# Loads of x alternating between two DMA rings in a rotary-embedding kernel

## The chip, the cores and the metric

One core of one Trainium2 chip. Times are device microseconds of whole executions; the profile's span is some 1.8 us shorter. The kernels of one round run on the same chip as the kernel before; the rounds used several chips, so compare ratios rather than medians.

In the profiles VectorE is DVE, ScalarE is ACT, GpSimd is POOL, TensorE is PE and SyncE is SP. A ring is the queue of transfers that one engine has issued, q1 for SyncE and q10 for ScalarE; the core's 16 DMA engines work on both. The granted clock is the share of its full clock at which TensorE was let run.

## The reference

```python
half = x.shape[-1] // 2                     # x: (8, 8, 1024, 64) float32
x_first, x_second = x[..., :half], x[..., half:]
out_first  = x_first * cos_cached - x_second * sin_cached   # tables: (1024, 32)
out_second = x_first * sin_cached + x_second * cos_cached
return concatenate([out_first, out_second], axis=-1)
```

16.8 MB come in, 16.8 MB go out; the tables are 128 KB each.

## The kernel before

x is cut into 16 chunks of 1 MiB, c0 to c15, each 128 partitions by 2048 values. All of x fits in SBUF, so every load has its own tile and none waits for a buffer. They are issued at the start, all on SyncE's ring, behind the sine table:

```python
nc.sync.dma_start(out=sn[0:Q], in_=sin_cached...)
nc.scalar.dma_start(out=cs[0:Q], in_=cos_cached...)
xt = []
for first, n in [(0, 1), (1, 1)] + [(c, 2) for c in range(2, n_ch, 2)]:
    t = xp.tile([P, n, F], fp32, name=f"x{first}")
    nc.sync.dma_start(out=t, in_=xf[first:first + n].rearrange("c p m -> p c m"))
    xt += [t[:, i] for i in range(n)]
```

So c0 and c1 are loads of one chunk, then come seven pairs. The tables are copied to all partitions (VectorE makes `snp`, ScalarE `csp`, GpSimd its own `sn` and `cs`). Then the chunks are dealt out (cuts marked by ...):

```python
vector_tensor(0); on_pool(1); vector_pool(2); vector_pool(3); vector_tensor(4)
on_pool(6); vector_pool(5); vector_tensor(7); vector_pool(8); ...
vector_tensor(11); vector_pool(12); vector_pool(13); vector_pool(14, ...); vector_alone(15)
```

VectorE makes two products for every chunk but c1 and c6, which GpSimd does alone. One product goes to a buffer `vs` (six of them), the other overwrites x. The sums are made by GpSimd (`vector_pool`, stored through SyncE), by TensorE with ScalarE copying them out of the PSUM tile `acc` (`vector_tensor`, stored through ScalarE), or by VectorE (`vector_alone`, only c15, whose product goes to `acc`).

## Time and profile before

| | before |
|---|---|
| median of 6 runs | 86.13 us (85.78 to 86.45) |
| profiled span | 84.2 us |
| VectorE, GpSimd busy | 84%, 85% |
| HBM traffic | 33.82 MB, mean 402 GB/s |
| first VectorE product, last VectorE instruction ends | 8.87, 77.19 us |
| last store lands | 83.1 us |

Read it from both ends. In the middle both the DMA engines and VectorE are full, so it isn't plain which of them sets the time. At the end VectorE is done six us before the last store has landed.

### The profile page before, as it was taken

How to read it: one execution, taken by the hardware profiler on the slowest of the kernel's cores; microseconds unless marked ns; L12 is line 12 of the kernel's file. 1: busy time of each engine (PE TensorE's matmuls, PEld its weight loads, DVE VectorE, ACT ScalarE, POOL GpSimd, SP SyncE). 2: the span in 40 equal slices, each digit the busy share in tenths (PEclk: the TensorE clock that was granted, in tenths of full speed). 3: DMA queues.
4: the chain of work that ended last, by engine and by line, in shares of the span. 5: the costliest groups of instructions: out<-in, count | busy, mean ns of one | idle time of the engine just before them, and what ended most of it. 6: DMA issues, size and time to landing. Idle time of an engine off the chain costs nothing.

```text
span 84.2 us, 363 instructions
## 1 busy us (share of the span) xinstructions
PE 40.1 (48%) x80; PEld 15.7 (19%) x80; DVE 70.4 (84%) x34; ACT 15.7 (19%) x16; POOL 71.4 (85%) x38
## 2 busy tenths in 40 slices
PE   0000005994930896895949497794949600000000
PEld 0000002422400341423314051332414100000000
DVE  0199997999999999999999982999999999996000
ACT  4399000004040003104040402204040310000000
POOL 3199999999999999999999999999999999970000
PEclk9999999999999569999999999999999999555555
DMA  3899999999999999999999999999999999999991
GB/s 29 282 432 409 420 420 436 417 409 420 436 428 409 417 428 432 432 424 409 421 436 436 432 421 417 424 424 436 432 432 432 413 421 428 428 436 407 432 419 55
DMA packets 4736, 33.82 MB, mean 402 GB/s; under 512 B 448, under 2 KB 448, under 8 KB 768
## 3 DMA queue, kind: packets, MB, share of 16 engines
q1 hardware_dynamic: 3824, 27.40, 78.7%
q10 hardware_dynamic: 912, 6.42, 18.1%
HBM read 17.04 MB, written 16.78 MB: 402 GB/s over the span
## 4 chain that ended last, share of the span: by engine, by line
POOL 53%; DVE 23%; issue 9%; DMA 4%; DVEq 1%; POOLq 0%
POOL x L94 13%; POOL x L93 11%; DVE vs L88 11%; POOL x L89 11%; POOL gs L88 11%; DVE x L89 8%; POOL sn L77 4%; DMA sn<-in_sin_cached_dram 4%; POOL cs L77 3%; DVE acc L88 3%; DVE x L93 1%; DVEq L170 1%; POOLq L93 0%; POOLq L77 0%
## 5 line engine op out<-in xcount | busy, mean ns | idle before, releaser
L119 PE MATMUL acc<-x,plus 128*128 128x512 f32 x40 | 23.3, 666 | 26.4 <-DVE x L89 13.6
L89 DVE TENSOR_TENSOR x<-x,csp 128x2048 f32<-128x2048 f32 x14 | 32.0, 2287 | 0.6
L88 DVE TENSOR_TENSOR vs<-x,snp 128x2048 f32<-128x2048 f32 x13 | 29.7, 2282 | 2.2 <-POOL x L94 1.7
L122 ACT COPY x<-acc 128x1024 f32<-128x1024 f32 x10 | 10.1, 1012 | 49.2 <-PE acc L120 49.2
L94 POOL TENSOR_TENSOR x<-x,vs 128x1024 f32<-128x1024 f32 (+1 forms) x9 | 19.0, 2108 | 0.0
L93 POOL TENSOR_TENSOR x<-x,vs 128x1024 f32<-128x1024 f32 (+1 forms) x9 | 18.9, 2105 | 0.0
L119 PEld LDWEIGHTS acc<-x,plus 128*128 128x128 f32 x40 | 7.5, 208 | 39.4 <-issue 23.9
L120 PE MATMUL acc<-vs,minus 128*128 128x512 f32 x20 | 11.6, 666 | 0.0
L120 PE MATMUL acc<-vs,plus 128*128 128x512 f32 x20 | 10.2, 592 | 0.0
L89 POOL TENSOR_TENSOR x<-x,cs 128x2048 f32<-128x2048 f32 x2 | 9.1, 4546 | 0.2
L88 POOL TENSOR_TENSOR gs<-x,sn 128x2048 f32<-128x2048 f32 x2 | 9.1, 4542 | 0.1
L73 DVE COPY snp<-sn 32x1024 f32<-32x1024 f32 x4 | 4.9, 1223 | 3.9 <-DMA sn<-in_sin_cached_dram 3.8
L120 PEld LDWEIGHTS acc<-vs,minus 128*128 128x128 f32 x20 | 4.4, 219 | 5.9 <-issue 5.9
L77 POOL COPY sn<-sn 32x1024 f32<-32x1024 f32 x3 | 3.1, 1032 | 2.7 <-DMA sn<-in_sin_cached_dram 2.6
L93 POOL TENSOR_TENSOR x<-x,gs 128x1024 f32<-128x1024 f32 x2 | 4.7, 2362 | 0.2
L94 POOL TENSOR_TENSOR x<-x,gs 128x1024 f32<-128x1024 f32 x2 | 4.7, 2357 | 0.0
L120 PEld LDWEIGHTS acc<-vs,plus 128*128 128x128 f32 x20 | 3.8, 190 | 4.8 <-issue 4.8
L74 ACT COPY csp<-cs 32x1024 f32<-32x1024 f32 x4 | 4.0, 1008 | 1.5 <-DMA cs<-in_cos_cached_dram 1.4
L77 POOL COPY cs<-cs 32x1024 f32<-32x1024 f32 x3 | 3.1, 1033 | 0.1
L88 DVE TENSOR_TENSOR acc<-x,snp 128x2048 f32<-128x2048 f32 x1 | 2.3, 2297 | 0.0
L71 ACT ACT_TABLE_LOAD x1 | 1.3, 1283 | 1.2 <-PEq L159 1.2
L93 DVE TENSOR_TENSOR x<-x,acc 128x1024 f32<-128x1024 f32 x1 | 1.2, 1223 | 0.0
(8 smaller groups left out, 2.4 us busy)
## 6 DMA issues: line engine op xcount, KB each, us to landing
x<-in_x_dram SPq DMA_DIRECT2D x7, 2048.0 KB, 25.0
out_dram<-x SPq DMA_DIRECT2D x9, 1024.0 KB, 13.0
out_dram<-x ACTq DMA_DIRECT2D x6, 1024.0 KB, 9.0
x<-in_x_dram SPq DMA_DIRECT2D x2, 1024.0 KB, 6.3
out_dram<-x SPq DMA_DIRECT2D x2, 512.0 KB, 6.0
cs<-in_cos_cached_dram ACTq DMA_DIRECT2D x1, 128.0 KB, 3.4
sn<-in_sin_cached_dram SPq DMA_DIRECT2D x1, 128.0 KB, 3.1
```

The costliest lines, as they stand in the source:

```text
L71: nc.scalar.mul(minus, plus, -1.0)
L73: nc.vector.tensor_copy(out=snp[r * Q:(r + 1) * Q], in_=sn[0:Q])
L74: nc.scalar.copy(out=csp[r * Q:(r + 1) * Q], in_=cs[0:Q])
L77: nc.gpsimd.tensor_copy(out=t[r * Q:(r + 1) * Q], in_=t[0:Q])
L88: eng.tensor_tensor(out=rows(s), in0=xr, in1=tab(stab), op=TT.mult)
L89: eng.tensor_tensor(out=xr, in0=xr, in1=tab(ctab), op=TT.mult)
L93: eng.tensor_tensor(out=xr[:, :, 0], in0=xr[:, :, 0], in1=sr[:, :, 1], op=TT.subtract)
L94: eng.tensor_tensor(out=xr[:, :, 1], in0=xr[:, :, 1], in1=sr[:, :, 0], op=TT.add)
L119: nc.tensor.matmul(a[:, k], plus, xr[:, :, k], start=True, stop=False)
L120: nc.tensor.matmul(a[:, k], plus if k else minus, sr[:, :, 1 - k], start=False, stop=True)
L122: nc.scalar.copy(out=xr, in_=a.rearrange("p k n j -> p n k j"))
L170: with _tile.TileContext(nc) as tc:
```

## The change

Its intent: two rings instead of one for the loads, so that the issues are spread over two engines and ACT's ring, nearly idle at first, carries half. The tables stay first on their rings.

```diff
     xt = []
-    for first, n in [(0, 1), (1, 1)] + [(c, 2) for c in range(2, n_ch, 2)]:
+    loads = [(0, 1), (1, 1)] + [(c, 2) for c in range(2, n_ch, 2)]
+    for i, (first, n) in enumerate(loads):
         t = xp.tile([P, n, F], fp32, name=f"x{first}")
-        nc.sync.dma_start(out=t, in_=xf[first:first + n].rearrange("c p m -> p c m"))
+        (nc.scalar if i % 2 else nc.sync).dma_start(
+            out=t, in_=xf[first:first + n].rearrange("c p m -> p c m"))
         xt += [t[:, i] for i in range(n)]
```

## The prediction

> **What bounds the kernel now.** I read the page's slices first, then the DMA issues, then VectorE in order of time, then the end. The work is 16 chunks of x of 1 MiB each (call them c0 to c15), in nine loads: c0, c1, then pairs (c2+c3, c4+c5, ... c14+c15). From part 2 of the page:
>
> ```profile
> DVE  0199997999999999999999982999999999996000
> POOL 3199999999999999999999999999999999970000
> DMA  3899999999999999999999999999999999999991
> GB/s 29 282 432 409 420 420 436 417 409 420 436 428 409 417 428 432 432 424 409 421 436 436 432 421 417 424 424 436 432 432 432 413 421 428 428 436 407 432 419 55
> ```
>
> The DMA engines are full from the second slice to the last but one, at 410 to 436 GB/s, so no other ring can move bytes faster: 33.82 MB at some 425 GB/s are 79.6 of the 84.2 us. But VectorE (DVE) is also full from the sixth slice to the 37th, apart from one hole, and GpSimd (POOL) beside it. Two bounds lie a few us apart, and what matters is when the first chunks arrive, because every us that VectorE loses early has to be found again.
>
> The issue of the second and third pair's loads, from the timeline of SyncE (start, duration), and their landings from the DMA view of the same moments (last number: us from issue to landing):
>
> ```profile
> 2.11 0.43 SPq L65 DMA_DIRECT2D x<-in_x_dram  x1
> 2.58 0.67 SPq L65 DMA_DIRECT2D x<-in_x_dram  x1
> ```
> ```profile
> x<-in_x_dram SPq DMA_DIRECT2D x1, 2048.0 KB, 11.9
> x<-in_x_dram SPq DMA_DIRECT2D x1, 2048.0 KB, 16.3
> ```
>
> So c2+c3 land at 2.11 + 11.9 = 14.0 and c4+c5 at 2.58 + 16.3 = 18.9. The same view gives c0 at 1.18 + 5.3 = 6.5, c1 at 1.64 + 7.4 = 9.0, c6+c7 at 23.9, c8+c9 at 28.8. One ring delivers in the order of issue, a pair every 4.9 us. VectorE's timeline shows how close that runs to need:
>
> ```profile
> 8.87 2.29 DVE L88 TENSOR_TENSOR vs<-x,snp 128x2048 f32<-128x2048 f32 x1
> 11.26 2.29 DVE L89 TENSOR_TENSOR x<-x,csp 128x2048 f32<-128x2048 f32 x1
> 13.99 2.29 DVE L88 TENSOR_TENSOR vs<-x,snp 128x2048 f32<-128x2048 f32 x1 [0.44 <-DMA x<-in_x_dram]
> ...
> 51.98 2.29 DVE L88 TENSOR_TENSOR vs<-x,snp 128x2048 f32<-128x2048 f32 x1 [1.74 <-POOL x L94]
> ```
>
> VectorE multiplies c0 from 8.87, is done at 13.55 and takes c2 as it lands (0.44 us late). From there it works without a hole, two products of 2.29 us a chunk, but for 1.74 us before 51.98: there it reuses a buffer of `vs` that GpSimd frees at 51.95 (c5's sums). The last thing in the program is c15's store, from ScalarE's timeline and the DMA view:
>
> ```profile
> 77.22 0.34 ACTq L97 DMA_DIRECT2D out_dram<-x  x1
> ```
> ```profile
> out_dram<-x ACTq DMA_DIRECT2D x1, 1024.0 KB, 5.9
> ```
>
> It lands at 83.1, and the program ends 1.0 us later. In the last four us the DMA engines clear what was left of the other stores, then c15.
>
> **What the Trainium skill says.** "DMA: Bandwidth & Descriptors", section "Rules for kernel authors", says of spreading DMAs over the issuing engines for bandwidth that it "Doesn't help", it only saves issue time. The trace agrees as far as it goes: one ring alone holds 420 to 436 GB/s, and SyncE's issues cost 0.4 to 0.7 us each while the transfers take 4.9. The same page, section "Queues, rings and completion order", says that each DMA engine goes round its rows packet by packet. So two rings with work should get half each. Here is the stretch from 28.6 to 33.0 us, loads on SP's ring (q1) and c0's store on ACT's (q10), DMA view (packets, MB, share):
>
> ```profile
> q10 hardware_dynamic: 119, 0.97, 52.2%
> q1 hardware_dynamic: 112, 0.92, 49.2%
> ```
>
> Half and half: it agrees, and this is the fact on which the prediction rests. The same page, "Anatomy of one DMA", puts a fixed cost of some 2 us beside the bytes; the trace's own number is below.
>
> **The change, step by step.** It removes and adds no transfer. c0, c2+c3, c6+c7, c10+c11, c14+c15 stay on SP; c1, c4+c5, c8+c9, c12+c13 go to ACT.
>
> 1. *Arrivals.* The first loads now run side by side in twos. c0 and c1, 2 MiB together, are done when the second was before: both at about 9.0 instead of 6.5 and 9.0. VectorE wants c0 at 8.87, so it loses 0.1 us. Then c2+c3 share with c4+c5: both land when the later one did, 18.7 to 18.9. c2 thus comes 4.8 us later. c6+c7 and c8+c9 come at 28.8, c10 to c13 at about 39: all before anyone wants them (GpSimd takes c6 at 33.4; VectorE would reach c8 at 41.5 and c10 at 50.5).
>
> 2. *VectorE's new hole.* Free at 13.6, it gets c2 at 18.8: a wait of 5.2 us where there were 0.44, a shift of 4.8.
>
> 3. *What is taken back.* GpSimd's own order hardly notices: it takes c1 from 10.44 (landed 9.0, and sn and cs are copied until 10.36), c2's sums at 24.26 (products then done at 18.8 + 4.6 = 23.4), c3's at 28.8 (28.0), c6 at 33.4, c5 at 47.3. So c5's sums still end at 51.95, and VectorE, which would come to that buffer at 50.24 + 4.8 = 55.0, no longer waits there. 1.74 us are absorbed: the shift of c11 to c15 is 3.1. GpSimd's c12, c13, c14 follow VectorE closely (c12's products end at 61.11, its sums start at 61.19) and move by 3.0 too.
>
> 4. *TensorE and ScalarE.* Their chunks c4, c7, c9, c11 run back to back, two copies of 1.01 us and two gaps of 3.79 each, 9.6 us a chunk, from c4's products on. They shift by 4.8: the last copy ends at 67.57 + 4.8 = 72.4. VectorE's c15 needs that PSUM tile at 70.18 + 3.1 = 73.3. It holds by 0.9.
>
> 5. *Issues on ScalarE.* Four issues of some 0.45 us now precede its table load (1.28) and copies of cs (4.13 in all). The fourth may have to wait for a semaphore in use: before, the seventh load's issue took until 6.5 and the eighth's until 11.2. If it waits for the tables (4.1), the csp copies end at 10.3, before VectorE's second product at 11.26: nothing. If it waits for c0 (9.0), they end at about 15, the second product at about 17.3: inside the hole of step 2, still nothing.
>
> 6. *The end.* VectorE ends at 77.19 + 3.1 = 80.3, and c15's store goes out at 80.35. Before, this store queued behind others. Now the queue is nearly dry: at 425 GB/s a chunk takes 2.47 us, and by 68.9, when c12's store goes out, the engines have done some (68.9 - 3.1) / 2.47 = 26.7 of the 32.25 chunks of traffic, with 27.25 on offer (16 loads, 0.25 of tables, 11 stores). From there they wait for work. For a lone 1 MiB I take c0's load: 5.3 us from issue, less 0.6 for the 256 KB of tables ahead of it, 4.7. So c15 lands between 84.4 (bytes start 1.0 after issue, 0.5 after the last one) and 80.35 + 4.7 = 85.1, against 83.1: plus 1.3 to 1.9.
>
> Sum: 4.8 lost, 1.7 taken back at the buffer, about 1.5 taken back from the store queue at the end; plus 1.6. 86.06 + 1.6 = 87.6 us, 1.8% more.
>
> **The rivals.** *Nothing moves (86.1).* "DMA bound, same bytes": for it, the DMA row of nines. Against it, c2's wait is visible already and VectorE has only 1.74 us of idle time from there on. It would come true if loads went to one ring first, c2 landing near 14. *The change pays (84 to 85).* It would have to come from SyncE's issues, which block until 11 and 15 us; but the ring is full then and the bytes flow at 425. c1 earlier would help GpSimd, but it starts on its table copies' end. I give this almost nothing. *A heavier loss (89 to 95).* If ScalarE's queue is held by a load's issue until c2 lands, csp is done only near 25, and VectorE shifts another 8. Or ACT's stores, now behind ACT's loads, hold back a semaphore or an issue that the PE chain needs; step 4 has 0.9 to spare. Possible, not likely.
>
> **Range and chances.** Step 2 is worth 4 to 5, depending on how evenly the rings share; step 6 takes back 1 to 2. That makes +0.7 to +2.4, and I widen the upper side for step 5: 86.7 to 88.9. The limit of 2% is 87.78, just above my middle: 0.42 slower, 0.56 within, 0.02 faster.
>
> **What would show it.** In the profile after: VectorE's wait for x before c2 about 5 us, starting 13.6; loads of the first two pairs landing within 0.3 us of each other near 18.8; no wait for GpSimd near 52; c15's store issued at 80.3; DMA under 9 tenths in slices near 73 and 80 us. The prediction fails if c2 lands near 14 (rings not shared), if ScalarE's csp copies come after 15, or if the last store lands later than 4.8 us after its issue.

## More of the kernel before

The chain that ended last, by engine, is from the page:

```profile
POOL 53%; DVE 23%; issue 9%; DMA 4%; DVEq 1%; POOLq 0%
```

It runs through GpSimd's work until 52 us and then through VectorE's. It stops at the last instruction and says nothing of the DMA queue behind the stores; for that one needs the row of DMA slices.

## The result, and the profile after

87.26 us (median of 6, 86.89 to 87.34) against 86.13 of the same rounds. The ratio is 1.0121 (95% interval 1.0089 to 1.0154). The change is slower, clear of the noise but by less than 2%, and inside the predicted range (86.7 to 88.9).

The page's slices after, the same rows as in the prediction:

```profile
DVE  0299993019999999999999999999999999999600
POOL 3199899999999999999999999999708999997000
DMA  2999999999999999999999999999999998699992
GB/s 56 310 424 431 416 412 427 427 420 431 427 408 420 424 420 427 431 424 404 424 431 431 427 424 427 431 424 431 431 431 431 431 427 377 289 393 422 379 408 85
```

VectorE has a hole in slices 7 to 9 (12.8 to 19.2 us) that wasn't there, and none any more in the middle. (GpSimd's new one, 2.9 us before 64.1, is its wait for c12's products, which VectorE now makes later.) The DMA engines are as full as before from the third slice on, at 404 to 431 GB/s (before 407 to 436), until the slices from 70 to 75 us, where they run short (289 GB/s at the worst). No bandwidth was won at the start; some was lost at the end.

The second and third pair's loads are now issued at the same moment, from SyncE's and ScalarE's timeline, and these are their landings in the DMA view:

```profile
1.65 0.43 SPq L66 DMA_DIRECT2D x<-in_x_dram  x1
```
```profile
1.66 0.46 ACTq L66 DMA_DIRECT2D x<-in_x_dram  x1
```
```profile
x<-in_x_dram SPq DMA_DIRECT2D x1, 2048.0 KB, 17.1
x<-in_x_dram ACTq DMA_DIRECT2D x1, 2048.0 KB, 18.7
```

c2+c3 land at 1.65 + 17.1 = 18.7 instead of 14.0. c4+c5 land at 20.4 instead of 18.9. Neither pair came sooner. (Only c12+c13, 40.3 instead of 41.1, and c14+c15, 46.0 instead of 48.8, did, long before they were wanted.) What the two rings moved from 5 to 18.7 us, in the DMA view (packets, MB, share):

```profile
q10 hardware_dynamic: 385, 2.91, 50.8%
q1 hardware_dynamic: 386, 2.90, 50.6%
```

It is half each. In the kernel before, q1 alone moved 5.78 MB in the same stretch. VectorE's timeline (start, duration, in brackets the idle time before and what ended it):

```profile
8.88 2.29 DVE L90 TENSOR_TENSOR vs<-x,snp 128x2048 f32<-128x2048 f32 x1
11.28 2.29 DVE L91 TENSOR_TENSOR x<-x,csp 128x2048 f32<-128x2048 f32 x1
18.75 2.29 DVE L90 TENSOR_TENSOR vs<-x,snp 128x2048 f32<-128x2048 f32 x1 [5.18 <-DMA x<-in_x_dram]
...
54.92 2.28 DVE L90 TENSOR_TENSOR vs<-x,snp 128x2048 f32<-128x2048 f32 x1
```

c0 is worked on at the same time as before. c2 starts at 18.75 instead of 13.99, 4.76 later. c11 starts at 54.92 instead of 51.98 and has no wait before it: 1.8 of the 4.76 has been absorbed. VectorE's last instruction ends at 80.12, 2.93 later than before. The last store, from ScalarE's timeline and the DMA view:

```profile
80.15 0.34 ACTq L99 DMA_DIRECT2D out_dram<-x  x1
```
```profile
out_dram<-x ACTq DMA_DIRECT2D x1, 1024.0 KB, 3.9
```

It lands at 84.0, 3.9 us after its issue where it took 5.9, because less is queued ahead of it: beside c15's own 1.05 MB SyncE's ring moved 0.20 MB from 80.2 us to the end, where before it moved 1.00 MB from 77.5 us on. That gives back another 2.0, and 0.9 of the 4.76 is left in the profile. The chain that ended last names the culprit now, in its summary by engine:

```profile
DVE 60%; DMA 20%; issue 11%; DVEq 1%; SPq 1%
```

The 20% of DMA is one piece, c2+c3's load from 1.65 to 18.73; from there it is VectorE to the end. GpSimd left the chain.

### The profile page after: what moved, and what is told of

Read it like the earlier page. It is cut to its first block, busy times and chain, and to the rows that moved or that the text cites. A ratio compares the mean times of both kernels' runs of the same rounds, so it can differ in the third digit from the quotient of the medians.

```text
span 85.1 us, 366 instructions
## 1 busy us (share of the span) xinstructions
PE 40.7 (48%) x80; PEld 15.9 (19%) x80; DVE 70.3 (83%) x34; ACT 15.7 (19%) x16; POOL 71.3 (84%) x38
## 4 chain that ended last, share of the span: by engine, by line
DVE 60%; DMA 20%; issue 11%; DVEq 1%; SPq 1%
DVE vs L90 32%; DVE x L91 24%; DMA x<-in_x_dram 20%; DVE acc L90 3%; DVE x L95 1%; DVEq L172 1%; SPq L66 0%; SPq L58 0%
## 5 line engine op out<-in xcount | busy, mean ns | idle before, releaser
L121 PE MATMUL acc<-x,plus 128*128 128x512 f32 x40 | 23.9, 682 | 30.5 <-DVE x L91 13.7
L124 ACT COPY x<-acc 128x1024 f32<-128x1024 f32 x10 | 10.1, 1012 | 51.9 <-PE acc L122 51.9
L96 POOL TENSOR_TENSOR x<-x,vs 128x1024 f32<-128x1024 f32 (+1 forms) x9 | 18.9, 2104 | 0.0
L122 PE MATMUL acc<-vs,plus 128*128 128x512 f32 x20 | 10.2, 592 | 0.0
```

What stands on the lines that cost most here:

```text
L96: eng.tensor_tensor(out=xr[:, :, 1], in0=xr[:, :, 1], in1=sr[:, :, 0], op=TT.add)
L121: nc.tensor.matmul(a[:, k], plus, xr[:, :, k], start=True, stop=False)
L122: nc.tensor.matmul(a[:, k], plus if k else minus, sr[:, :, 1 - k], start=False, stop=True)
L124: nc.scalar.copy(out=xr, in_=a.rearrange("p k n j -> p n k j"))
```

## The experiments

The theory: c2 comes late because the DMA engines share themselves between rings that have work, whatever it is; VectorE's late start is the cost, less what two slacks give back. Rivals: the second ring or ScalarE's issues cost by themselves; the order of the stores; the neighbour c4+c5 in particular.

**One load moved.** c1 alone on ACT's ring, ratio 0.9995 [0.9978, 1.0012], 85.94 us.

```diff
-        (nc.scalar if i % 2 else nc.sync).dma_start(
+        (nc.scalar if i == 1 else nc.sync).dma_start(
```

> Only c1's load goes to ACT's ring; every pair stays on SP. Theory (c2 comes late because it shares the DMA engines with another pair): c0 and c1 share, c0 lands near 8.8 instead of 6.5, but c2+c3 have the engines to themselves and land at 14.0 as before; VectorE's wait before c2 stays under 0.6 us; time as before, 86.1 (85.8 to 86.4). Rival (a second ring in use, or load issues on ScalarE, costs by itself): a good part of the 1.1 us of the change is there, 86.5 or more.

```profile
13.81 2.29 DVE L90 TENSOR_TENSOR vs<-x,snp 128x2048 f32<-128x2048 f32 x1 [0.27 <-DMA x<-in_x_dram]
```

c0 landed at 8.8 and c2 was taken at 13.81. Using the second ring for one load, with c0 sharing with c1, costs nothing that these runs can tell.

**Another neighbour.** c4+c5 back on SyncE, so that c2+c3 runs beside c8+c9. 88.41 us, ratio 1.0279 [1.0246, 1.0312].

```diff
-        (nc.scalar if i % 2 else nc.sync).dma_start(
+        (nc.scalar if i in (1, 5, 7) else nc.sync).dma_start(
```

> The change, but c4+c5 go back to SP, so that c2+c3's neighbour on ACT's ring is c8+c9. Theory (any bytes on the other ring take half): c2+c3 still land at 18.8, VectorE still waits 5.2 us, and now c4+c5, which share with c12+c13, land near 28.7 while VectorE is free at 27.9: 0.8 more. Time 88.1 (87.6 to 88.5), slower than the change. Rival (it was the pair c4+c5 itself, next in order, that held c2 up): c2 lands near 14, time near 86.1.

```profile
18.84 2.29 DVE L90 TENSOR_TENSOR vs<-x,snp 128x2048 f32<-128x2048 f32 x1 [5.03 <-DMA x<-in_x_dram]
...
28.78 2.29 DVE L90 TENSOR_TENSOR vs<-x,snp 128x2048 f32<-128x2048 f32 x1 [0.81 <-DMA x<-in_x_dram]
```

c2 is as late as in the change, and c4 is late too, by the 0.8 us foreseen. Not foreseen was that GpSimd waited 2.9 us for c6+c7, which landed at 36.4. Its neighbour was not a load any more (c12+c13 had landed at 29.4), but c0's store on ACT's ring, issued at 25.0 and landed at 34.6. The time is 0.3 above the middle of the forecast.

**A load that nobody wants early.** Only c12+c13 on ACT's ring. 88.22 us, ratio 1.0274 [1.0237, 1.0310].

```diff
-        (nc.scalar if i % 2 else nc.sync).dma_start(
+        (nc.scalar if i == 7 else nc.sync).dma_start(
```

> Of all loads only c12+c13 goes to ACT's ring, 2 MiB that nobody wants before 58 us; c0, c1, c2 ... stay in order on SP. Theory (c2 is late by the bytes that another ring moves before it): c0 lands near 8.9, c1 and c12+c13 near 13.9, c2+c3 near 18.8, VectorE waits 5 us as in the change; GpSimd also gets c1 3.5 us late. VectorE ends near 80.6, time 87.5 (87.0 to 88.0). Rival (the alternation of neighbours costs, one load that is wanted late does not): 86.0 to 86.3.

```profile
19.06 2.29 DVE L90 TENSOR_TENSOR vs<-x,snp 128x2048 f32<-128x2048 f32 x1 [5.41 <-DMA x<-in_x_dram]
```
```profile
14.23 4.50 POOL L90 TENSOR_TENSOR gs<-x,sn 128x2048 f32<-128x2048 f32 x1 [3.75 <-DMA x<-in_x_dram]
```

The clearest run of all: one transfer of 2 MiB on an otherwise idle ring delays all that SyncE's ring holds until it has landed (at 15.7 us), and both VectorE and GpSimd wait. The mechanism was as forecast, the size was not: VectorE ended at 81.2, not 80.6, since c2 came 0.3 later than foretold, and c11 and c15 waited 0.3 and 0.4 us for GpSimd and ScalarE. The median is 0.2 above the range. It mixes two groups: 87.86 to 87.92 us at a granted clock of 0.894 to 0.910, inside the range, and 88.53 to 88.73 at 0.881 to 0.882, of which the profile is one. The last experiments come back to these groups.

**Alternation without the harm.** c2 to c5 as single chunks, so that c2's neighbour is c3; the last load of ACT after its `csp` copies.

```diff
-    loads = [(0, 1), (1, 1)] + [(c, 2) for c in range(2, n_ch, 2)]
+    loads = [(c, 1) for c in range(6)] + [(c, 2) for c in range(6, n_ch, 2)]
     ...                      # loads[9] = c12+c13: issued after the csp copies
```

> The rings still alternate, but c2, c3, c4, c5 are loads of one chunk each, so that what shares with c2 is c3, which VectorE wants next (ACT's last load, c12+c13, is issued after the csp copies so that ScalarE isn't held). Theory: c2 and c3 land at 13.8 to 15.4, c4 and c5 at 18.7 to 20.4; VectorE's wait before c2 is under 0.7 us and no other wait for x appears; time 86.1 (85.8 to 86.5). Rival (alternation costs by itself, through uneven rings or later stores): 86.9 or more.

```profile
14.22 2.29 DVE L96 TENSOR_TENSOR vs<-x,snp 128x2048 f32<-128x2048 f32 x1 [0.21 <-DMA x<-in_x_dram]
```

85.97 us, ratio 0.9994 [0.9977, 1.0010]. All loads still alternate. What shares with c2 is what comes next, both land near 14.2 to 14.5, and the loss is gone. (The edit has two parts, smaller loads and a later c12+c13; no run has them apart.)

**The hole alone.** The kernel before with one ring, VectorE making c2's first product three times.

```diff
-        eng.tensor_tensor(out=rows(s), in0=xr, in1=tab(stab), op=TT.mult)
+        for _ in range(3 if c == 2 else 1):
+            eng.tensor_tensor(out=rows(s), in0=xr, in1=tab(stab), op=TT.mult)
```

> The kernel before with all loads on SP, but VectorE makes c2's first product three times (the same values, 2.28 us each), so that its later work shifts by 4.56 us with the rings untouched. Theory (the late start of VectorE is the whole cost): no wait for GpSimd near 52, VectorE ends at 80.0, c15's store lands near 83.9, time 87.1 (86.8 to 87.3), about the change's 87.3. Rival (a part of the cost comes from the loads and stores in other rings): 86.1 to 86.5.

```profile
14.04 6.93 DVE L89 TENSOR_TENSOR vs<-x,snp 128x2048 f32<-128x2048 f32 x3 [0.40 <-DMA x<-in_x_dram]
```

86.90 us, ratio 1.0119 [1.0086, 1.0153], the same as the change's 1.0121, with every load on SyncE's ring and c2 at hand at 14.0. At like clocks (0.908 to 0.912) it took 86.63 to 86.82 and the change, run again below, 86.87 to 86.95, with the kernel before at 86.0 in both; its shift is 0.2 us shorter. So the lost VectorE time explains the cost, to the 0.2 us or so that these runs can tell; the rings and the stores' order need add nothing. With one extra product instead of two (`2 if c == 2`):

> As the run with two extra products on VectorE, but one: a shift of 2.28 us. Theory (the wait of 1.74 us for GpSimd near 52 takes up the first 1.74 us, and the queue of stores at the end the rest): VectorE ends 0.5 us later than before, the last store lands within 0.3 us of before; time 86.1 (85.9 to 86.35). Rival (cost in proportion to the shift, half of the 0.9 of two extra products): 86.45.

86.04 us, ratio 1.0021 [1.0003, 1.0040]. VectorE ended at 78.2, 1.0 us later than before (0.5 foreseen, and a wait of 0.7 for ScalarE before c15 not foreseen), at almost no cost. The cost is not in proportion to the shift.

**VectorE faster, before.** `bufs=7` instead of 6 for `vs` in the kernel before.

> The kernel before with seven buffers of vs instead of six. Theory (before ends with the DMA engines, VectorE has slack): the wait of 1.74 us for GpSimd near 52 goes or moves, VectorE ends up to 1.7 us earlier, near 75.5, the last store still lands near 83, time 86.0 (85.7 to 86.2). Rival (VectorE's stream sets the time before too): 84.3 to 84.8.

86.05 us, ratio 1.0010 [0.9991, 1.0030]. The wait near 52 was gone, VectorE ended at 75.2, and c15's store went out 2.0 us earlier and took 1.9 us longer:

```profile
out_dram<-x ACTq DMA_DIRECT2D x1, 1024.0 KB, 7.8
```

The time is the same, so the store waited the longer for what was queued ahead of it. The kernel before ends with the DMA engines; VectorE has slack.

**ACT's loads late.** As the change, but ACT issues its pairs only after its `csp` copies (shortened).

```diff
+        if i % 2 and i > 1:
+            late.append((q, t, first, n))     # issued after the csp copies
+        else:
+            q.dma_start(...)
```

> The change's rings, but ACT issues c4+c5, c8+c9, c12+c13 only after its csp copies, near 8.5 us, so that c2+c3 runs alone until about 11. Theory: c2+c3 lands at 15.5 to 17, VectorE's wait before c2 is 2 to 3.5 us, of which the buffer wait near 52 gives back 1.74 and the end of the queue most of the rest: 86.2 (85.9 to 86.5). Rival (the rings' alternation costs whenever the loads are issued): 87.2 as the change.

A miss: 88.44 us (four executions), ratio 1.0294 [1.0275, 1.0314]. c2+c3 landed at 16.9 as worked out and VectorE waited 3.2 us for it, also as worked out. But it then stood still a second time:

```profile
52.08 2.29 DVE L96 TENSOR_TENSOR vs<-x,snp 128x2048 f32<-128x2048 f32 x1 [3.42 <-POOL x L102]
```

That is c10's product, not c11's. GpSimd's sums of c5 end at 51.9 in the kernel before, 52.0 in the change and 52.1 here, and here c10 waits for them; in the change c10 started at 50.40, before they ended. So the program as built gives c5's buffer to c10 here (read from the waits, as the views leave buffer numbers out): with the order of issue, the order in which buffers are handed out had changed. The same kernel with seven buffers:

> The run with ACT's pairs issued after the csp copies, but seven buffers of vs. That run came out at 88.4, not 86.2: c2 landed at 16.9 and the wait was 3.2 us, as forecast, but VectorE then waited 3.4 us for GpSimd at 52.1, one chunk earlier than in the kernel before, because the program as built hands c5's buffer to c10 instead of c11. Theory (that wait is the miss): with a seventh buffer it goes, VectorE ends near 78.3, time 86.2 (85.9 to 86.6). Rival (the late rings themselves cost 2 us): 87.5 or more.

86.17 us (five executions), ratio 1.0013 [1.0001, 1.0025]: the second wait gone, the first still 3.1 us. VectorE ended at 78.9, not 78.3, with a wait of 0.8 us for ScalarE before c15 that was not foreseen, and the kernel is 0.1 us slower than before. So the buffer wait was the miss, and a hole of 3 us at the start is nearly free.

**Buffers in the changed kernel.** `bufs=7` in the change:

> The changed kernel with seven buffers of vs. Theory: the change has no buffer wait any more, so a seventh buffer has nothing to remove: VectorE ends at 80.1 again, time 87.2 (86.9 to 87.4). Rival (buffers still hold the changed kernel up somewhere): under 86.8.

87.55 us, ratio 1.0168 [1.0131, 1.0205]; the changed kernel in the same rounds 87.02, ratio 1.0135 [1.0107, 1.0163]. No gain, as forecast, and not below 86.8; but a median above the range, which leads to the last question.

**Two groups of times.** The changed kernel again:

> The changed kernel once more, beside the next three on the same chip: 87.2 (86.9 to 87.4), VectorE waiting 5.2 us for c2. Its six runs fell in two groups before, 86.9 at a granted clock of 0.909 and 87.2 to 87.3 at 0.876 to 0.895; if the lower clock delays the chunks on TensorE by over the 0.8 us that c15's product has to spare, a profile of the second group shows VectorE waiting for ScalarE before c15.

Its runs: 86.87 to 86.95 at a granted clock of 0.911 to 0.912, then 87.09, 87.14 (0.893) and 87.75 (0.879). The kernel before in these rounds: 85.91 to 86.06 at clocks from 0.882 to 0.916, with no such order. The profile taken was of the faster group, so it couldn't show the slower. The test of my explanation:

```diff
-        products(nc.vector, c, acc, csp, snp)
-        sums(nc.vector, c, acc, 0, R)
+        s = tv.tile([P, F], fp32, name="vs")
+        products(nc.vector, c, s, csp, snp)
+        sums(nc.vector, c, s, 0, R)
```

> The changed kernel with c15's products in an SBUF buffer of vs instead of the PSUM tile that ScalarE reads last. Theory (the two groups of times are c15 waiting for ScalarE when TensorE's clock was lower for longer): all runs in the lower group, 86.9 (86.7 to 87.1). Rival (the groups have another source, or the PSUM tile never matters): both groups again, median 87.2.

The explanation fell: 87.63 us, ratio 1.0192 [1.0179, 1.0205], all four executions at 0.876 to 0.882, although c15 could no longer wait for ScalarE; the unedited change took 87.75 at such a clock (0.879). (The edit isn't quite neutral: one of c15's sums took 1.68 us instead of 1.22.) The traces suggest another. When TensorE's clock stays low longer as c4 begins after a pause, c4, c7, c9 and c11 all come later. The rows of granted clock from the two pages, the change first, this run below:

```profile
PEclk9999999999999755699999999999999999995555
```
```profile
PEclk9999999999999555559999999999999999965555
```

The dip before the middle (slices of 2.1 us) reads 7, 5, 5, 6 in the first and five times 5 in the second, and c4's first copy out of PSUM starts at 37.6 and 39.2. The issue of c11's store, from ScalarE's timeline, and the windows view from 70 to 74 us (columns after the window: its length, busy time of PE, PEld, DVE, ACT, POOL, clock, DMA share, GB/s), first the change, then this run:

```profile
72.31 0.34 ACTq L99 DMA_DIRECT2D out_dram<-x  x1
```
```profile
70.00:74.00 4.00, 1.23 (x3) 0.19 (x1) 3.93 (x3) 1.01 (x1) 4.00 (x3) 1.00 0.82 332
```
```profile
73.83 0.34 ACTq L99 DMA_DIRECT2D out_dram<-x  x1
```
```profile
70.00:74.00 4.00, 2.75 (x7) 0.95 (x5) 3.96 (x3) 1.01 (x1) 4.00 (x3) 1.00 0.63 264
```

With c11's store 1.5 us later the DMA engines, already dry, move 264 GB/s instead of 332 in that stretch, and the last store lands 4.4 us after its issue instead of 3.9. Two more profiles fit: c11's store at 72.62 and 3.9 us for the last one in the change's second profile (0.912), 73.32 and 4.4 us with seven buffers (0.877). The kernel before has 430 GB/s there and doesn't feel the clock. No run moved c11's store by itself, so this part is argued from traces, not shown.

No version beat the kernel before by more than its spread: the best, c1 alone on ACT (0.9995) and single chunks (0.9994), equal it.

## Why the prediction was right

The runs, put in order of when VectorE ends in the profile, show the shape that the prediction worked out from two slacks:

| kernel | VectorE ends, us | c15's store lands (after its issue), us | median, us |
|---|---|---|---|
| before, 7 buffers | 75.2 | 83.0 (7.8) | 86.05 |
| before | 77.2 | 83.1 (5.9) | 86.0 |
| one extra product | 78.2 | 83.1 (4.9) | 86.04 |
| ACT late, 7 buffers | 78.9 | 83.3 (4.3) | 86.17 |
| change | 80.1 | 84.0 (3.9) | 87.02, 87.26 |
| two extra products | 80.2 | 84.7 (4.5) | 86.90 |
| c4+c5 on SP | 81.1 | 85.3 (4.2) | 88.41 |
| only c12+c13 on ACT | 81.2 | 85.5 (4.3) | 88.22 |
| ACT late | 81.8 | 85.7 (3.9) | 88.44 |

The second and third columns are of the profiled execution. For two extra products and for only c12+c13 that was one of the slower ones, at a low clock (87.57 us at 0.876, 88.72 at 0.882), so their landings are late for the medians beside them. The landing is flat while the DMA engines end last, and rises once c15's store is the last to come: 83.1, where the last store landed before, less the 3.9 of a nearly lone store is 79.2, between the fourth line and the fifth.

- *Steps 1 and 2* held where they matter: c0 usable at 8.8, c2 at 18.7, a wait of 5.18, a shift of 4.76 (4.8). The detail that both pairs land within 0.3 us failed: ACT's landed 1.6 later than SP's in this profile (0.6 in the second one of the same kernel), and c1 came at 10.5 instead of 9.0. It cost GpSimd 0.3 us and nothing at the end.
- *Step 3* held: no wait near 52, shift of c11 2.94 (3.1).
- *Step 4* held in both profiles of the changed kernel: c11's last copy ended at 72.3 and 72.6, c15 started at 73.1. Its spare was as thin as said; with seven buffers a profile shows a wait of 0.2.
- *Step 5* held: ACT's fourth load waited for its own table, until 4.1, and the `csp` copies ended at 10.2 (10.3).
- *Step 6* was right in kind and mis-sized. c15's store landed 3.9 us after its issue, where I had 4.1 to 4.7, the upper one taken from c0's load. So the profile shows plus 0.9 instead of 1.3 to 1.9, and the time plus 1.1 instead of 1.6. The dry stretch near 73 was there; the one near 80 was not.
- Of the rivals, "nothing moves" is what the DMA engines give with c2 near 14, as the runs with c1 alone and with single chunks show. The heavier loss (89 to 95) came in no run. Its first cause, late `csp` copies, did not occur. Its second did in part: c0's store, ready at 25.5, stood in ScalarE's queue until 30.4, just after c8+c9 had landed on the same ring (30.3). It cost nothing, since ScalarE's next copy began only at 37.6.
- Readings that were loose, without consequence: the second slice of the kernel before is 8 tenths full, at 282 GB/s, and the full ones reach down to 407; issues of 0.4 to 0.7 us are only SyncE's first six; and 80.35 + 4.7 is 2.0 after 83.1, not 1.9.

## What to carry to other kernels

Where one ring already fills the DMA engines, as here, a second ring added no bandwidth and took away the order: a transfer on the idle ring took half of the DMA engines from whatever waited on the other (2.91 of 5.81 MB), wanted or not. If loads must be spread, pair on the two rings what is wanted at the same time, and in pieces as small as the first consumer's, as the single chunks did. Before pricing a delay at an engine's start, follow it to the end through every slack; and after changing the order of issues, check that buffers are still handed out as before.

## What the Trainium skill lacked or had wrong

- "DMA: Bandwidth & Descriptors", "Rules for kernel authors": it says that spreading DMAs over issuing engines for bandwidth doesn't help. It doesn't say that it can hurt by delaying what is needed first: c2 at 18.7 instead of 14.0 us, 1.2% of the time; with one late-needed load of 2 MiB on the other ring 2.7%.
- The same page, "Queues, rings and completion order", describes taking turns by packet; it doesn't say how close together two equal neighbours land. In the change ACT's 2 MiB landed 0.6 and 1.6 us after SP's in two profiles, issued 0.01 us apart.
- The same page, "Anatomy of one DMA", fits 2.0 us of fixed cost plus the bytes at 436 GB/s to DMAs that GpSimd issues, by which I estimate 4.4 us for 1 MiB. It has no such fit for DMAs that ScalarE or SyncE issue; a store of 1 MiB from ScalarE with little ahead of it landed in 3.9 us here.
- I found no page that says how much a ring takes before an issue stands still. In the kernel before, the first six loads (10 MiB) were issued in under 0.7 us each, the seventh took 2.16 and the eighth 4.62; with the loads split over two rings none took over 0.51, though SyncE's fifth first waited 6.3 us for an earlier load to land (in the kernel before, its ninth waited 2.8).
